# Gate/up stage of a two-layer encoder: left operands, right sides and products of its first units in another order

## The chip, the cores and the metric

The kernel runs on one core of a Trainium2 chip. Its time is the device time of one execution in microseconds. The engines are named as the profile names them: PE is TensorE (matmuls; PEld is its loading of weights), DVE is VectorE, ACT is ScalarE, POOL is GpSimd, and SP is SyncE, which here only issues DMAs.

## The reference

Two layers, each with an attention part and a SwiGLU part, on a sequence of 1024 tokens with 1024 features, all in float32. The change lies in the part below; the attention part only delivers `concat(y_tok, y_mem)`. D_FF is 2816.

```python
def rmsnorm(x, g):
    x32 = x.astype(jnp.float32)
    y = x32 * lax.rsqrt(jnp.mean(x32 * x32, axis=-1, keepdims=True) + EPS)
    return (y * g.astype(jnp.float32)).astype(x.dtype)
...
    for i in range(DEPTH):
        ...
        x = x + jnp.concatenate([y_tok, y_mem], axis=-1) @ w_out[i]
        h = rmsnorm(x, norm_ffn[i])
        gu = h @ w_gate_up[i]
        x = x + (jax.nn.silu(gu[..., :D_FF]) * gu[..., D_FF:]) @ w_down[i]
    return rmsnorm(x, norm_final)
```

## The kernel before

Activations lie transposed: a tile `x[m][f]` holds 128 features (m = 0..7) by 512 tokens (f = 0, 1). A float32 operand is split in two parts of a type that PE takes, `hi` (a cast on ACT, L106) and `lo` (the rest, a subtraction on DVE, L109), and a product is the sum of three matmuls, hi·hi, hi·lo and lo·hi.

Behind the attention each layer has three stages. The **output projection** makes `x[m][f]` for both halves of the tokens, eight products of 24 matmuls for each half. Its weights `wo` are loaded into raw buffers (tag `raw`, five of them, shared with the later stages) and split into left operands (tag `whl`, three buffers). In the second half each product is also followed by the normalizing of one tile of the first half and by its split into `hB`, the right sides B[0] and B[1].

The **gate/up stage** has 22 units (class `Pair`). A unit makes 128 rows of gate and 128 of up, as a product of a 2 by 2 block matrix (g1, g2, u1, u2) with a 2 by 2 block matrix (b11, b12, b21, b22), in seven products instead of eight (Strassen in Winograd's form). Product n takes a left operand and a right side B[n]:

- n = 0, 1: g1 and g2, with b11 and b21
- n = 2, 3: S2 = u1 + u2 - g1 and S1 = u1 + u2, with T2 = b22 - T1 and T1 = b12 - b11
- n = 4, 5: S3 = g1 - u1 and S4 = g2 - S2, with T3 = b22 - b12 and b22
- n = 6: u2, with T4 = T2 - b21

A product is 12 matmuls into a PSUM bank: 0, 2, 4 and 6 into the unit's `X`, 1, 3 and 5 into a `Y`, of which there are three. `read(n)` takes the result out: ACT copies `X` or a `Y`, or DVE adds it to an earlier copy. `prepare(n)` makes the left operands of n and n + 1 in one tile `wgu` of tag `whl`: for n = 0 from the raw gate weights, for n = 2 and 4 from a tile `wS` (tag `S`, two buffers) that POOL fills in two operations of 128 x 512, for n = 6 from u2. Each of the two raw tiles of a unit is 512 KB; after n = 4 and n = 6 a call of `load_gu` issues a next one on SP.

`right_sides()` normalizes the second half of the tokens: the sums of squares are finished (on PE, `st`), a power is taken on POOL (`nr`, L217), PE spreads it to all partitions (`bc`), and DVE scales the tiles x[k][1] by it. It then makes T2, T1, T3, b22 and T4 in this order, each for four blocks k, as `hT` or `hB`; a call of `run_some(rest, 3)` does three of its 20 steps.

The order of the products is a list: products 0 and 1 of units 0 to 3 (which need B[0] and B[1] alone), then products 2 to 6 of unit 0, of unit 1, of unit 2, of unit 3, then units 4 to 21, seven products each. `gate_up()` goes through the list; `prepare` runs four entries ahead. The order of instructions on an engine is set by a scheduler that goes by the order of the program and by what is ready, and is fixed when the kernel is built. All of the first left operands, five loads and four calls of `prepare`, stand in the program behind the output projection.

The **down stage** follows; its right sides come from DRAM tiles that `hand_over` writes after every second unit.

Of the kernel before, what the change touches and what calls it, by code (L numbers as in the profile page):

```python
# [17 lines left out]
P = 128  # L18
# [23 lines left out]
def trunk_kernel(ctx: ExitStack, tc: tile.TileContext, a: dict, out: bass.AP):  # L42
# [62 lines left out]
    def hi(dst, src):  # L105
        nc.scalar.copy(dst, src)  # L106
# [224 lines left out]
    for layer in range(2):  # L331
# [427 lines left out]
        with tc.tile_pool(name=f"fp{layer}", bufs=1, reuse_waits="tile") as fp:  # L759
# [27 lines left out]

            for m in range(3):
                load_x(m, 0)
            for f in range(2):  # L790
                for m in range(NK):
# [17 lines left out]
                    if f == 1:  # L809
                        k = next(parts)  # L810
                        B[k // 4][k % 4] = pair(x[k][0], h_op(k))

            def right_sides():

                bc = norms[1].scale()
                sub = lambda o, p_, q_: nc.vector.tensor_tensor(o, p_, q_, op=ALU.subtract)
                for k in range(4):
                    b11, b12, b21, b22 = x[k][0], x[k][1], x[k + 4][0], x[k + 4][1]
                    for i, t in ((k, b12), (k + 4, b22)):
                        nc.vector.scalar_tensor_tensor(  # L820
                            t, t, gains[:, 2 + layer, i : i + 1], bc, op0=ALU.mult, op1=ALU.mult
                        )
                    sub(b11, b12, b11)
                    t2 = temp("t2")
                    sub(t2, b22, b11)
                    B[2][k] = pair(t2, t_op(k))
                    sub(b21, t2, b21)
                    yield
                for k in range(4):
                    B[3][k] = pair(x[k][0], t_op(k))  # L830
                    yield
# [4 lines left out]
                for k in range(4):  # L836
                    B[5][k] = pair(x[k + 4][1], h_op(k))
                    yield
                for k in range(4):
                    B[6][k] = pair(x[k + 4][0], h_op(k))  # L840
                    yield

            class Pair:


                def __init__(self, j):
                    self.j = j
                    self.left, self.raw = {}, {}

                def prepare(self, n):  # L850

                    if n % 2 == 1:
                        return
                    g1, g2 = self.raw[0][:, :HS], self.raw[0][:, HS:]
                    if n > 0:
                        u1, u2 = self.raw[1][:, :HS], self.raw[1][:, HS:]
                    sub = lambda o, p_, q_: nc.gpsimd.tensor_tensor(o, p_, q_, op=ALU.subtract)
                    s = self.raw[0]
# [10 lines left out]
                    if n == 6:  # L869
                        hi(w[:, 0, :HS], u2)  # L870
                        lo(w[:, 1, :HS], u2, w[:, 0, :HS])
                    else:
                        hi(w[:, 0], s)
                        lo(w[:, 1], s, w[:, 0])
                    self.left[n], self.left[n + 1] = w[:, :, :HS], w[:, :, HS:]
                    if n > 3:
                        load_gu()

                def product(self, n):
                    if n == 0:  # L880
                        self.X = (
                            ps_s.tile([P, HS], F32, tag="S", name="X")
                            if self.j % 2
                            else ps_mm.tile([P, HS], F32, tag="mm", name="X")
                        )
                    if n in (1, 3):
                        self.Y = ps_t.tile([P, HS], F32, tag="T", name="Y")
                    ps, w = (self.Y if n in (1, 3, 5) else self.X), self.left[n]
                    for k in range(4):
                        kw = (w[:, 0, k * P : (k + 1) * P], w[:, 1, k * P : (k + 1) * P])  # L890
                        for i, (l, r) in enumerate(three(kw, (B[n][k][:, 0], B[n][k][:, 1]))):
                            nc.tensor.matmul(  # L892
                                ps, l, r, start=n in (0, 1, 3, 6) and k == 0 and i == 0,
                                stop=k == 3 and i == 2, skip_group_check=True,
                            )

                def read(self, n):
                    X, Y = self.X, getattr(self, "Y", None)
                    add = lambda o, p_, q_, op=ALU.add: nc.vector.tensor_tensor(o, p_, q_, op=op)  # L899
# [64 lines left out]
            for _ in range(5):  # L964
                load_gu()
# [301 lines left out]
```

## Time and profile before

| | |
|---|---|
| time, median of 3 runs (lowest to highest) | 2222.61 us (2220.63 to 2223.34) |
| time of the profiled execution | 2225.55 us |
| its span (first to last instruction) | 2223.8 us |
| mean granted clock of PE | 0.983 of full speed |
| PE busy | 2134.8 us, 96% |
| PEld busy | 1751.2 us, 79% |
| DVE busy | 1515.4 us, 68% |
| ACT busy | 1058.1 us, 48% |
| POOL busy | 692.1 us, 31% |

Busy time is the union of an engine's instructions; weight loads run beside matmuls and have their own line. A share is a mean over all stages of both layers. A wait is idle time of an engine directly ahead of an instruction, put down to the instruction that released it. The times in the rows further on count from the start of the span. In the timelines a row gathers neighbouring instructions of one kind, with the start of the first and the time that they took together.

### The profile page before, as it was taken

To read this page: it belongs to the slowest core of one execution; us is meant where nothing else is said; L and a number is where in the kernel's file an instruction comes from. 1 tells how busy PE (TensorE), PEld (TensorE's weight loads), DVE (VectorE), ACT (ScalarE), POOL (GpSimd) and SP (SyncE) were. 2 spreads that over 40 slices of the span, in tenths; PEclk is the share of its full clock that TensorE was granted. 3 is DMA by queue.
4 is the path that set the end of the run, shared out by engine and by line. 5 is a ranking of instruction groups with operands and counts; after the bars stand their busy time and mean duration, and the time that the engine had idled before them with its cause. 6 is when DMAs were issued, how large, how long until landed. Compare 5 with 4: busy or idle time off the path is not lost.

```text
span 2223.8 us, 28171 instructions
## 1 busy us (share of the span) xinstructions
PE 2134.8 (96%) x9930; PEld 1751.2 (79%) x9930; DVE 1515.4 (68%) x2241; ACT 1058.1 (48%) x2016; POOL 692.1 (31%) x647
## 2 busy tenths in 40 slices
PE   6899999899999999999999999999999999999996
PEld 6788888778888887787778888887788888877775
DVE  5677786776656665767866666667866566657575
ACT  5477784443333333445466566644433333334442
POOL 5334330143323330363233223201433333303540
PEclk9999999989999999999999999999999999999998
DMA  6312118223323236756332222282233332366562
GB/s 232 105 53 73 43 58 284 85 90 109 108 97 113 87 114 227 246 200 216 112 101 69 76 68 74 62 277 91 90 106 108 100 107 92 110 231 227 174 225 89
DMA packets 116444, 285.11 MB, mean 128 GB/s; under 512 B 12240, under 2 KB 18640, under 8 KB 116304
## 3 DMA queue, kind: packets, MB, share of 16 engines
q1 hardware_dynamic: 109968, 271.79, 36.5%
q10 hardware_dynamic: 6336, 11.54, 1.4%
q8 instruction: 78, 1.28, 0.2%
q14 instruction: 62, 0.51, 0.1%
HBM read 208.30 MB, written 68.94 MB: 125 GB/s over the span
## 4 chain that ended last, share of the span: by engine, by line
PE 39%; DVE 4%; issue 3%; ACT 2%; DMA 2%; POOL 1%; SPq 0%; POOLq 0%; DVEq 0%; ACTq 0%
PE X L892 10%; PE mm L139 8%; PE Y L892 8%; PE po L139 4%; PE X L1116 2%; PE Y L1116 2%; PE S L524 2%; PE O L587 2%; DMA b_raw<-b_d 1%; PE pT L567 1%; DVE hB L109 1%; DVE wd L109 1%; ACT wd L106 0%; ACT p L539 0%; DVE sq L202 0%
## 5 line engine op out<-in xcount | busy, mean ns | idle before, releaser
L892 PE MATMUL X<-hT,wgu 128*128 128x512 f32 x1056 | 265.5, 399 | 5.6 <-ACT wgu L106 4.0
L892 PE MATMUL Y<-hB,wgu 128*128 128x512 f32 x1056 | 257.8, 392 | 10.7 <-DVE g L899 10.7
L1116 PE MATMUL X<-hB,wd 128*128 128x512 f32 x1056 | 249.2, 396 | 8.2 <-ACT hB L106 3.6
L892 PE MATMUL X<-hB,wgu 128*128 128x512 f32 x1056 | 251.6, 393 | 0.0
L892 PEld LDWEIGHTS X<-hT,wgu 128*128 128x128 f32 x1056 | 200.3, 190 | 55.2 <-ACT wgu L106 4.8
L1116 PEld LDWEIGHTS X<-hB,wd 128*128 128x128 f32 x1056 | 200.8, 191 | 54.3 <-ACT hB L106 4.4
L892 PEld LDWEIGHTS Y<-hB,wgu 128*128 128x128 f32 x1056 | 199.1, 189 | 55.0 <-DVE g L899 11.6
L862 POOL TENSOR_TENSOR wS<-wgu_raw 128x512 f32<-128x512 f32 x44 | 73.0, 1659 | 536.0 <-issue 416.9
L552 POOL TENSOR_SCALAR p<-p,stat 128x384 f32<-128x384 f32 (+1 forms) x256 | 140.9, 570 | 309.8 <-DVE stat L549 206.7
L892 PEld LDWEIGHTS X<-hB,wgu 128*128 128x128 f32 x1056 | 200.3, 190 | 43.0 <-DVE wgu L109 1.3
L139 PE MATMUL mm<-hT,wqk 128*128 128x512 f32 x672 | 200.0, 405 | 0.1
L1116 PE MATMUL Y<-hB,wd 128*128 128x512 f32 x792 | 183.6, 392 | 9.3 <-DVE hB L109 4.5
L109 DVE TENSOR_TENSOR wgu<-wgu_raw,wgu 128x1024 fp32r<-128x1024 f32 (+1 forms) x88 | 98.6, 1121 | 135.1 <-ACT wgu L106 135.1
L139 PE MATMUL po<-yT,wo 128*128 128x512 f32 x768 | 184.7, 394 | 0.0
L1116 PEld LDWEIGHTS Y<-hB,wd 128*128 128x128 f32 x792 | 149.4, 189 | 42.5 <-DVE hB L109 5.3
L109 DVE TENSOR_TENSOR hB<-b_raw,hB 128x512 fp32r<-128x512 f32 x154 | 130.5, 884 | 63.0 <-ACT hB L106 62.8
L106 ACT CAST wgu<-wS 128x1024 fp32r<-128x1024 f32 x88 | 92.5, 1051 | 156.9 <-PE Y L892 104.8
L139 PEld LDWEIGHTS po<-yT,wo 128*128 128x128 f32 x768 | 142.4, 188 | 29.6 <-issue 1.0
L109 DVE TENSOR_TENSOR wgu<-wS,wgu 128x1024 fp32r<-128x1024 f32 x88 | 146.9, 1670 | 25.2 <-ACT wgu L106 25.2
L106 ACT CAST wgu<-wgu_raw 128x1024 fp32r<-128x1024 f32 (+1 forms) x88 | 73.4, 834 | 181.6 <-PE Y L892 131.7
L106 ACT CAST hB<-b_raw 128x512 fp32r<-128x512 f32 x154 | 88.9, 619 | 104.3 <-DMA b_raw<-b_d 104.1
L539 ACT ACTIVATE p<-p,stat 128x256 f32<-128x256 f32 (+1 forms) x192 | 112.3, 586 | 51.3 <-DVE stat L535 48.8
(162 smaller groups left out, 4053.6 us busy)
## 6 DMA issues: line engine op xcount, KB each, us to landing
wgu_raw<-in_w_gu SPq DMA_DIRECT2D x88, 512.0 KB
b_raw<-b_d SPq DMA_DIRECT2D x70, 512.0 KB
wd_raw<-in_w_dn SPq DMA_DIRECT2D x50, 512.0 KB
b_d<-c SPq DMA_DIRECT2D x88, 256.0 KB
b_d<-t SPq DMA_DIRECT2D x66, 256.0 KB
wo_raw<-in_w_out SPq DMA_DIRECT2D x32, 512.0 KB
wd_kept<-in_w_dn SPq DMA_DIRECT2D x10, 1024.0 KB
x<-in_x SPq DMA_DIRECT2D x32, 256.0 KB
```

What stands on the lines that cost most here:

```text
L106: nc.scalar.copy(dst, src)
L109: (eng or nc.vector).tensor_tensor(dst, src, h.bitcast(F32), op=ALU.subtract)
L139: nc.tensor.matmul(ps[:, :n], l, r, start=start and i == 0 and j == 0, stop=stop and i == len(order) - 1 and j == 2,)
L524: nc.tensor.matmul(s_[:, :n], Q[self.h][:, qb * P : (qb + 1) * P], k, start=j == 0, stop=j == 1)
L539: nc.scalar.activation(p[:, :n], p[:, :n], AF.Exp, bias=m1, scale=-1.0, accum_out=s1)
L552: nc.gpsimd.tensor_scalar(p[:, :n], p[:, :n], ri[:, i : i + 1], 1.0, op0=ALU.mult, op1=ALU.mult)
L567: nc.tensor.transpose(tr[:, j * P : (j + 1) * P], p[:, j * P : (j + 1) * P], ident)
L587: nc.tensor.matmul(o[:, c0 : c0 + w * P], self.value(j), t[:, s0 : s0 + w].rearrange("p j q -> p (j q)"), start=j == js[0] and t is self.p ...
L862: nc.gpsimd.tensor_tensor(s[:, HS:], u1, u2, op=ALU.add)
L892: nc.tensor.matmul(ps, l, r, start=n in (0, 1, 3, 6) and k == 0 and i == 0, stop=k == 3 and i == 2, skip_group_check=True,)
L1116: nc.tensor.matmul(bank, l, r, start=i in (0, 1, 3, 6) and p == 0 and n == 0, stop=p == HF - 1 and n == 2, skip_group_check=True,)
```

## The change

The class `Pair`, the list of units and the list of loads move ahead of the output projection. In the second half of the projection (f = 1) the loop also loads gate and up weights and, at m = 2 to 5, calls `prepare(0)` of units 0 to 3; these four operands lie in tiles `wgu8` of tag `t8` instead of `whl`. The up weights of units 0 and 1 are loaded there too; units 2 and 3 load their gate weights a second time later.

`prepare` rounds n down to an even number and returns where that operand has been made. For n = 4 it doesn't take a new `wS` tile: S3 and S4 overwrite S1 and S2 in the tile of n = 2, S4 in place, in halves that are swapped.

`right_sides` goes in the order T1, T2, b22, T3, T4. A tile of the second half is scaled where it is first needed (x[k][1] for T1, x[k+4][1] for T2); T2 takes the place of T1 in x[k][0] instead of a temporary tile. One of its steps runs ahead of the first product, then one after each of the first eight products and two after each later one.

The order of products 2 to 6 of the early units goes by pairs, units 0 and 1 and then units 2 and 3: product 3 of both, then 2, 5, 4, 6 of both. In `read` the multiplication of c2 by g2 stands with whichever of products 4 and 5 comes last. The number of matmuls, casts, subtractions and right sides is what it was.

```diff
+                def prepare(self, n):
+
+                    n -= n % 2
+                    if n in self.left:
+                        return
 ...
-                    if n in (2, 4):
-                        s = fp.tile([P, D], F32, tag="S", name="wS", bufs=2)
-                    if n == 2:
-                        nc.gpsimd.tensor_tensor(s[:, HS:], u1, u2, op=ALU.add)
-                        sub(s[:, :HS], s[:, HS:], g1)
-                        self.s2 = s[:, :HS]
-                    if n == 4:
-                        sub(s[:, :HS], g1, u1)
-                        sub(s[:, HS:], g2, self.s2)
-                    w = wp.tile([P, 2, D], F32R, tag="whl", name="wgu", bufs=3)
+                    if n == 2:
+                        self.s = fp.tile([P, D], F32, tag="S", name="wS", bufs=2)
+                    if n in (2, 4):
+                        s = self.s
+                    if n == 2:
+                        nc.gpsimd.tensor_tensor(s[:, HS:], u1, u2, op=ALU.add)
+                        sub(s[:, :HS], s[:, HS:], g1)
+                    if n == 4:
+                        sub(s[:, HS:], g1, u1)
+                        sub(s[:, :HS], g2, s[:, :HS])
+                    if n == 0 and self.j < first:
+                        w = fp.tile([P, 2, D], F32R, tag="t8", name="wgu8", bufs=6)
+                    else:
+                        w = wp.tile([P, 2, D], F32R, tag="whl", name="wgu", bufs=3)
 ...
+                    if n == 4:
+                        self.left[4], self.left[5] = self.left[5], self.left[4]
-                    if n > 3:
+                    if n > 3 or (n == 0 and 2 <= self.j < first):
                         load_gu()
 ...
                         add(self.c2, self.c2, self.c1)
+                        if 5 in self.seen:
+                            add(self.c2, self.c2, self.g2, ALU.mult)
 ...
-            order += [(u, n) for u in us[:first] for n in range(2, 7)]
+            for j in range(0, first, 2):
+                order += [(u, n) for n in (3, 2, 5, 4, 6) for u in us[j : j + 2]]
-            loads = [(u, 0) for u in us[:first]] + [(u, 1) for u in us[:first]]
-            loads += [(u, i) for u in us[first:] for i in range(2)]
+            loads = [(us[j], 0) for j in range(first)] + [(us[0], 1), (us[1], 1)]
+            loads += [(u, i) for u in us[2:] for i in range(2)]
 ...
                         B[k // 4][k % 4] = pair(x[k][0], h_op(k))
+                        if 1 <= m <= 2:
+                            load_gu()
+                        if 2 <= m < 2 + first:
+                            if m == 4:
+                                load_gu()
+                            if m == 3:
+                                load_gu()
+                            us[m - 2].prepare(0)
 ...
+                for k in range(4):
+                    t = x[k][0]
+                    sub(t, normalized(k), t)
+                    B[3][k] = pair(t, t_op(k))
+                    yield
+                for k in range(4):
+                    t, b21 = x[k][0], x[k + 4][0]
+                    sub(t, normalized(k + 4), t)
+                    B[2][k] = pair(t, t_op(k))
+                    sub(b21, t, b21)
+                    yield
+                for k in range(4):
+                    B[5][k] = pair(x[k + 4][1], h_op(k))
+                    yield
 ...
-            for _ in range(5):
-                load_gu()
-            lead = 4
-            for u, n in order[:lead]:
-                u.prepare(n)
+            lead = 4
+            rest = right_sides()
 ...
             def gate_up():
+                run_some(rest, 1)
+                load_gu()
 ...
-                    if i < 2 * first:
-                        run_some(rest, 3)
                     u.product(n)
                     u.read(n)
+                    run_some(rest, 1 if i < 2 * first else 2)
```

What this does to the engines' fixed orders, at three places of layer 0. In the rows a name left of the arrow is written, names right of it are read, and a number behind a name tells tiles of one name apart.

PE before, from the sixth product of the stage on (products 0 and 1 of the early units, then the first that take T2, `hT_4551` and `hT_4568`, and T1, `hT_4595` and `hT_4618`):

```order
L892 MATMUL Y<-hB,wgu 128x512 x12
L892 MATMUL X<-hB,wgu 128x512 x2
L892 MATMUL X<-hT_4551,wgu 128x512 x2
L892 MATMUL Y<-hB,wgu 128x512 x2
L892 MATMUL X<-hB,wgu 128x512 x10
L892 MATMUL Y<-hB,wgu 128x512 x10
L892 MATMUL Y<-hT_4595,wgu 128x512 x2
L892 MATMUL X<-hT_4551,wgu 128x512 x4
L892 MATMUL X<-hT_4568,wgu 128x512 x6
L892 MATMUL Y<-hT_4595,wgu 128x512 x4
L892 MATMUL Y<-hT_4618,wgu 128x512 x6
L892 MATMUL X<-hT_4624,wgu 128x512 x2
```

PE now, from the fifth product on (`wgu_4410` and `wgu_4454` are the first operands of units 2 and 3; `hT_4553` and `hT_4594` are T1, `hT_4633` and `hT_4686` T2):

```order
L844 MATMUL X<-hB,wgu_4410 128x512 x12
L844 MATMUL Y<-hB,wgu_4410 128x512 x12
L844 MATMUL X<-hB,wgu_4454 128x512 x12
L844 MATMUL Y<-hB,wgu_4454 128x512 x12
L844 MATMUL Y<-hT_4553,wgu 128x512 x6
L844 MATMUL Y<-hT_4594,wgu 128x512 x6
L844 MATMUL Y<-hT_4553,wgu 128x512 x6
L844 MATMUL Y<-hT_4594,wgu 128x512 x6
L844 MATMUL X<-hT_4633,wgu 128x512 x6
L844 MATMUL X<-hT_4686,wgu 128x512 x6
L844 MATMUL X<-hT_4633,wgu 128x512 x6
L844 MATMUL X<-hT_4686,wgu 128x512 x6
```

Products 0 and 1 of all four units now stand whole ahead of any product with a T, and product 3 of two units comes ahead of their product 2.

DVE before, where the T2 of layer 0 end and the T1 are split (`g1_4585` is the sum that reads unit 0's first `Y`, `wgu_4615` the first operand of unit 3, the `x` written by L816 first T2's and later T3's terms):

```order
L816 TENSOR_TENSOR x_3924<-x_4179,x_3924 128x512
L109 TENSOR_TENSOR hT8_4568<-t2_4566,hT8_4568 128x512
L816 TENSOR_TENSOR t2_4590<-x_4355,x_3924 128x512
L109 TENSOR_TENSOR hT8_4595<-x_3918,hT8_4595 128x512
L816 TENSOR_TENSOR x_4026<-t2_4590,x_4026 128x512
L109 TENSOR_TENSOR hT8_4568<-t2_4590,hT8_4568 128x512
L109 TENSOR_TENSOR hT8_4595<-x_3920,hT8_4595 128x512
L899 TENSOR_TENSOR g1_4585<-Y_4600,g1_4585 128x512
L109 TENSOR_TENSOR wgu_4615<-wgu_raw_4519,wgu_4615 128x1024
L109 TENSOR_TENSOR hT8_4618<-x_3922,hT8_4618 128x512
L109 TENSOR_TENSOR hT8_4618<-x_3924,hT8_4618 128x512
L816 TENSOR_TENSOR x_4063<-x_4233,x_4063 128x512
```

DVE now, from the first scaling of the right sides on (L936 scales, L933 subtracts, `hT8_4553` and `hT8_4594` are T1; `g1_4571` and `g1_4610` read the first `Y` of units 0 and 1):

```order
L936 SCALAR_TENSOR_TENSOR x_4063<-x_4063,gains_104,bc_4549 128x512
L936 SCALAR_TENSOR_TENSOR x_4100<-x_4100,gains_104,bc_4549 128x512
L933 TENSOR_TENSOR x_3918<-x_4063,x_3918 128x512
L933 TENSOR_TENSOR x_3920<-x_4100,x_3920 128x512
L852 TENSOR_TENSOR g1_4571<-Y_4577,g1_4571 128x512
L109 TENSOR_TENSOR hT8_4553<-x_3918,hT8_4553 128x512
L109 TENSOR_TENSOR hT8_4553<-x_3920,hT8_4553 128x512
L936 SCALAR_TENSOR_TENSOR x_4142<-x_4142,gains_104,bc_4549 128x512
L936 SCALAR_TENSOR_TENSOR x_4179<-x_4179,gains_104,bc_4549 128x512
L933 TENSOR_TENSOR x_3922<-x_4142,x_3922 128x512
L933 TENSOR_TENSOR x_3924<-x_4179,x_3924 128x512
L852 TENSOR_TENSOR g1_4610<-Y_4616,g1_4610 128x512
```

Before, the first of these sums stands behind 26 operations of the right sides; now behind four. No low part of a `wgu` stands between them.

POOL before, from the power of the first half's norm (`nr_4222`) past that of the second half (`nr_4539`); `wS_4667` and `wS_4721` belong to unit 0:

```order
L217 TENSOR_TENSOR nr_4222<-nv_4221,neg_half_109 128x4
L862 TENSOR_TENSOR wS_4667<-wgu_raw_4521 128x512
L857 TENSOR_TENSOR wS_4721<-wgu_raw_4513,wgu_raw_4521 128x512
L857 TENSOR_TENSOR wS_4667<-wS_4667,wgu_raw_4513 128x512
L857 TENSOR_TENSOR wS_4721<-wgu_raw_4513,wS_4667 128x512
L217 TENSOR_TENSOR nr_4539<-nv_4538,neg_half_109 128x4
L862 TENSOR_TENSOR wS_4784<-wgu_raw_4727 128x512
L857 TENSOR_TENSOR wS_4784<-wS_4784,wgu_raw_4515 128x512
```

POOL now, the same stretch; `wS_4637`, `wS_4663` and `wS_4873` belong to units 0, 1 and 2, and the second power is `nr_4544`:

```order
L803 TENSOR_TENSOR wS_4663<-wS_4663,wgu_raw_4316 128x512
L803 TENSOR_TENSOR wS_4637<-wgu_raw_4273,wgu_raw_4413 128x512
L803 TENSOR_TENSOR wS_4637<-wgu_raw_4273,wS_4637 128x512
L803 TENSOR_TENSOR wS_4663<-wgu_raw_4316,wgu_raw_4457 128x512
L803 TENSOR_TENSOR wS_4663<-wgu_raw_4316,wS_4663 128x512
L810 TENSOR_TENSOR wS_4873<-wgu_raw_4733 128x512
L803 TENSOR_TENSOR wS_4873<-wS_4873,wgu_raw_4556 128x512
L217 TENSOR_TENSOR nr_4544<-nv_4543,neg_half_109 128x4
L810 TENSOR_TENSOR wS_4895<-wgu_raw_4829 128x512
```

Ahead of the second power stood four operations on weights, of unit 0; now ten stand there, the last two of them for S1 and S2 of unit 2. S3 and S4 of a unit go into the tile of its S1 and S2.

## Rows read from the trace of the kernel before

**Rows 1.** Waits of PE: engine, tile, line, releaser: us in total, times, longest us

```profile
PE Y L892 <- DVE g L899: 10.7, 2, 5.3
...
PE X L892 <- ACT wgu L106: 4.0, 2, 3.3
...
PE X L892 <- DVE wgu L109: 1.6, 2, 1.3
```

**Rows 2.** Windows: window, us, busy us (count) of each engine, clock, DMA share, GB/s

```profile
418.62:437.83 19.21, 18.60 (x83) 14.64 (x82) 14.97 (x24) 7.28 (x10) 1.02 (x1) 1.00 0.04 14
437.83:469.50 31.67, 23.07 (x75) 17.21 (x74) 28.65 (x37) 17.40 (x29) 12.90 (x6) 0.78 0.10 34
513.29:532.58 19.29, 19.29 (x85) 15.77 (x84) 13.52 (x14) 7.07 (x10) 6.60 (x4) 1.00 0.35 124
1552.57:1582.21 29.64, 21.79 (x75) 15.67 (x74) 28.27 (x37) 17.39 (x29) 7.04 (x4) 0.83 0.06 17
```

**Rows 3.** Timeline of PE, layer 0: start, us, instruction, count, [wait, releaser]

```profile
418.62 4.01 PE L892 MATMUL X<-hB,wgu 128*128 128x512 f32 x17
...
437.83 0.61 PE L892 MATMUL X<-hB,wgu 128*128 128x512 f32 x2
...
444.26 1.22 PE L892 MATMUL Y<-hB,wgu 128*128 128x512 f32 x2 [5.35 <-DVE g L899]
...
461.24 5.49 PE L892 MATMUL X<-hT,wgu 128*128 128x512 f32 x12 [3.25 <-ACT wgu L106]
...
510.57 5.60 PE L892 MATMUL X<-hB,wgu 128*128 128x512 f32 x24
516.01 2.88 PE L892 MATMUL Y<-hB,wgu 128*128 128x512 f32 x12
```

**Rows 4.** Timeline of PE, layer 1, the same places

```profile
1533.36 4.01 PE L892 MATMUL X<-hB,wgu 128*128 128x512 f32 x17
...
1552.57 0.62 PE L892 MATMUL X<-hB,wgu 128*128 128x512 f32 x2
...
1628.73 2.88 PE L892 MATMUL Y<-hB,wgu 128*128 128x512 f32 x12
```

**Rows 5.** Timeline of DVE and POOL behind the stage's start, layer 0

```profile
419.96 1.23 DVE L109 TENSOR_TENSOR wgu<-wgu_raw,wgu 128x1024 fp32r<-128x1024 f32 x1 [0.44 <-ACT wgu L106]
...
423.96 1.02 POOL L217 TENSOR_TENSOR nr<-nv,neg_half 128x4 f32<-128x4 f32 x1 [8.92 <-DVE nv L216]
...
426.92 1.41 DVE L820 SCALAR_TENSOR_TENSOR x<-x,gains,bc 128x512 f32<-128x512 f32 x2 [1.22 <-PE bc L226]
...
444.12 1.22 DVE L109 TENSOR_TENSOR wgu<-wgu_raw,wgu 128x1024 fp32r<-128x1024 f32 x1
...
453.06 3.70 DVE L109 TENSOR_TENSOR hB<-x,hB 128x512 fp32r<-128x512 f32 x6
```

**Rows 6.** POOL's subtractions by line (ns: least/median/most), and timelines at units 0 and 5

```profile
L857 POOL TENSOR_TENSOR wS<-wgu_raw x44: 1282/1677/2282, 409.7 to 1939.1; 128x512 f32<-128x512 f32 x44
...
L857 POOL TENSOR_TENSOR wS<-wgu_raw,wS x44: 1290/1730/1748, 413.8 to 1940.7; 128x512 f32<-128x512 f32 x44
...
452.77 5.14 POOL L862 TENSOR_TENSOR wS<-wgu_raw 128x512 f32<-128x512 f32 x1 [27.79 <-DVE wgu L109]
...
551.86 1.63 POOL L862 TENSOR_TENSOR wS<-wgu_raw 128x512 f32<-128x512 f32 x1 [12.25 <-issue]
...
554.79 0.59 ACT L902 COPY g<-X 128x512 f32<-128x512 f32 x1 [1.59 <-PE X L892]
...
557.31 2.95 PE L892 MATMUL X<-hT,wgu 128*128 128x512 f32 x12
```

**Rows 7.** Timelines: cast of a `wo` operand on ACT, and a load and its first use

```profile
402.56 1.05 ACT L106 CAST wo<-wo_raw 128x1024 fp32r<-128x1024 f32 x1 [3.86 <-PE po L139]
...
463.52 0.88 SPq L962 DMA_DIRECT2D wgu_raw<-in_w_gu  x2
...
467.16 1.29 POOL L862 TENSOR_TENSOR wS<-wgu_raw 128x512 f32<-128x512 f32 x1 [3.67 <-DMA wgu_raw<-in_w_gu]
```

More of the change, by code (lines that the diff above doesn't have):

```diff
@@ new lines, in trunk_kernel @@
+            us = [Pair(j) for j in range(NF)]
+            first = 4
+            order = [(u, n) for u in us[:first] for n in (0, 1)]
+            for j in range(0, first, 2):
+                order += [(u, n) for n in (3, 2, 5, 4, 6) for u in us[j : j + 2]]
+            order += [(u, n) for u in us[first:] for n in range(7)]
+            loads = [(us[j], 0) for j in range(first)] + [(us[0], 1), (us[1], 1)]
+            loads += [(u, i) for u in us[2:] for i in range(2)]
+            loads = iter(loads)
@@ L788, in trunk_kernel, with load_gu @@
+            def load_gu():
+                u, i = next(loads, (None, 0))
+                if u is not None:
+                    u.raw[i] = raw_tile("wgu_raw")
+                    nc.sync.dma_start(u.raw[i], a["w_gu"][layer, 2 * u.j + i])
             for m in range(3):
@@ L816, in right_sides, with normalized @@
                 sub = lambda o, p_, q_: nc.vector.tensor_tensor(o, p_, q_, op=ALU.subtract)
-                for k in range(4):
[L818 to L827, printed above, removed]
+                def normalized(i):
+                    nc.vector.scalar_tensor_tensor(
+                        x[i][1], x[i][1], gains[:, 2 + layer, i : i + 1], bc, op0=ALU.mult, op1=ALU.mult
+                    )
+                    return x[i][1]
+                for k in range(4):
+                    t = x[k][0]
+                    sub(t, normalized(k), t)
+                    B[3][k] = pair(t, t_op(k))
                     yield
                 for k in range(4):
-                    B[3][k] = pair(x[k][0], t_op(k))
+                    t, b21 = x[k][0], x[k + 4][0]
[5 more added lines that the diff above has]
+                    B[5][k] = pair(x[k + 4][1], h_op(k))
                     yield
@@ L946, in hand_over @@
                 keep(6, p, o)
-            us = [Pair(j) for j in range(NF)]
-            first = 4
-            order = [(u, n) for u in us[:first] for n in (0, 1)]
-            order += [(u, n) for u in us[:first] for n in range(2, 7)]
-            order += [(u, n) for u in us[first:] for n in range(7)]
-            loads = [(u, 0) for u in us[:first]] + [(u, 1) for u in us[:first]]
-            loads += [(u, i) for u in us[first:] for i in range(2)]
-            loads = iter(loads)
-            def load_gu():
-                u, i = next(loads, (None, 0))
-                if u is not None:
-                    u.raw[i] = raw_tile("wgu_raw")
-                    nc.sync.dma_start(u.raw[i], a["w_gu"][layer, 2 * u.j + i])
-            for _ in range(5):
-                load_gu()
             lead = 4
-            for u, n in order[:lead]:
-                u.prepare(n)
             rest = right_sides()
             def gate_up():
+                run_some(rest, 1)
+                load_gu()
                 for i, (u, n) in enumerate(order):
```

125 lines of the change are left out of this document (60 added, 65 removed).

## The prediction

> **What bounds the kernel now.** I read the waits of PE first: in the gate/up stage it stood 10.7 us, in two waits, for an addition of VectorE (DVE) into `g`, and 5.6 us for left operands `wgu` [rows 1]. Two waits means one for each layer, so the loss sits at one place of a layer. The windows show where. The first 19.2 us of the stage run at full clock with PE at 18.60 of 19.21; the next 31.7 us have PE at 23.07, a mean granted clock of 0.78, which is a mix of the levels 1.2 and 2.4 GHz, and DVE busy 28.65 us; a later unit of 19.29 us has PE busy throughout [rows 2]. Layer 1 has the same hole (21.79 of 29.64, clock 0.83). So PE bounds the stage except in one stretch behind its start, which DVE sets.
>
> PE's own timeline says what it costs. Two products (24 matmuls) start at 510.57 and the next at 516.01, so a product takes 2.72 us; the first of these two ends the four early units, and unit 4 starts at 513.29 [rows 3]. The stage starts at 418.62: the four early units took 94.67 us. Four units at the later pace are 4 x 19.29 = 77.16 [rows 2]. Layer 1: start 1533.36, unit 4 at 1628.73 - 2.72 = 1626.01, so 92.65 us [rows 4]. The losses are 17.5 and 15.5 us. Of each, the first six products hold 2.9 (19.21 instead of 6 x 2.72 = 16.32, in both layers [rows 3, 4]): the sums of squares and the broadcast of the norm, which stay. What is left for the change is 94.67 - 19.21 - (77.16 - 16.32) = **14.6 us in layer 0 and 12.6 in layer 1**.
>
> Where these went: PE waits 5.35 us at 444.26 because the addition that frees a Y bank stands on DVE behind the right sides, and the left operand of unit 3 gets its low part only at 444.12 [rows 3, 5]. At 461.24 it waits again, 3.25 us, for a cast of S2, and the twelve matmuls behind take 5.49, twice their later 2.72, at the lower clock [rows 3].
>
> **The change part by part.**
>
> *Left operands of units 0 to 3 during the projection.* Four casts and four subtractions move ahead of the stage; in their old places stand the casts of S2 of units 0 and 1 and S3 of unit 0, which have no wait left. Low parts also leave the stretch in which DVE is the bound, such as that of unit 3 at 444.12 [rows 5]. Cost ahead: four times 1.05 on ScalarE (ACT) and 1.23 on DVE [rows 5, 7], beside a projection in which PE was never idle. The cover there is the lead of `wo`: the cast at 402.56 waited 3.86 us for PE to free its buffer [rows 7]; with 1.05 and 1.23 behind it, its operand is ready near 404.9 and used at 418.62 - 5.44 = 413.2, so 8.3 us ahead. The new loads take four of five raw buffers, so the last three `wo` loads go through one buffer in turn. A turn is the load (two were issued from 463.52 to 464.40, the data of the later was used at 467.16 [rows 7]; about 3 us), 1.05, 1.23 and about 0.7 of handing over: 6 us against PE's 5.44. Counting back three products from 404.9, the first of these turns begins near 388.6; the third ends near 406.6, still 6.6 us ahead. I price this at nothing. Two repeated loads for units 2 and 3 (512 KB each) fall into a stretch with a DMA share of 0.04 to 0.10 [rows 2]: nothing.
>
> *Right sides begun with T1.* The count is the same (44 operations of DVE, 0.62 us each by six in 3.70 us [rows 5], 27 us in all); only the order changes. They start 8.30 us after the stage's start [rows 3, 5]. The four T1 with two additions are 14 operations: done 17.0 after the start. PE needs them after eight products, 19.21 + 5.44 = 24.65. T2 with two additions is 18 more: 28.2, needed from 24.65 + 5.6 = 30.2. The four b22: 30.7, needed at 35.8. T3 and one subtraction for a left operand: 36.9, needed at 41.3. T4: about 40, needed at 46.8. The thinnest margin is 2.0 us, at T2, and its last quarter is needed 2 us later still. So DVE, today the bound, drops behind PE. Next late would be T2.
>
> *Pairs.* Two units take product 3, then 2, 5, 4, 6 in turn. A Y bank is freed by an addition that now stands between right sides: that of unit 0 comes fifth, after two scalings and two T1 differences, 2.5 us into them, and PE needs the bank 13 us later. Each left operand gets its buffer two products or more before its use, 5.4 us against 1.05 + 1.23. ACT copies c1 of the second unit about 1 us before PE overwrites X: no stall, but little room.
>
> *The norm behind two operations of GpSimd (POOL).* The power for the norm started at 423.96, when its input came [rows 5]. In the new order unit 2's sum and difference for S2 stand ahead of it, and they wait for the low part that ends at 419.96 + 1.23 = 421.2 [rows 5]. Two operations at 1.28 to 1.68 end at 423.8 to 424.6: the power comes 0 to 0.7 us later, and with it everything behind. I take **0.4 us in each layer**, the middle. Their data are in place: PE frees the buffer for S2 of unit 0 at 418.62 - 2 x 5.44 = 407.7; cast, subtraction and two POOL operations end near 413.4 and release the raw buffer, and a load of 3 us lands near 416.4.
>
> *S3 and S4 overwrite S2.* In the 18 later units of each layer the two subtractions for S3 and S4 can start only when DVE has read S2, at 551.86, where today an operation starts on the same release. They last 1.677 and 1.730 at the median [rows 6], so 555.27; the cast takes it to 556.32, the copy of X behind it on ACT (0.59) to 556.91. PE overwrites X at 557.31 [rows 6]. Today that copy starts at 554.79. So 0.40 us of room are left of 1.9, in every later unit: nothing, but the closest cover in the change. With the longest of the 44, 2.282 and 1.748, it is 0.22 late [rows 6].
>
> The Trainium skill (SBUF — State Buffer, "Who interferes with whom") says that a DVE instruction with two SBUF inputs and a GpSimd instruction that reads SBUF exclude each other, the later one blocking until the first is through. By that each subtraction waits for at most one DVE operation; those that stand there take 0.62, so 1.28 + 0.62 = 1.90 each and the copy ends at 557.30: the room is gone and nothing lost, 2196. Behind one of 1.23 it would be 0.60 late in 36 units, 2218. The medians of this trace lie below the first of these; one row of 5.14 beside six DVE operations [rows 5, 6] lies above both.
>
> **The sum.** 14.6 + 12.6 - 2 x 0.4 = 26.4 us. The profiled execution took 2225.55 (span 2223.8): 2199.1. It lies 0.13% above the median of 2222.61; scaled, **2196.2 us**.
>
> **The rivals.**
> (a) *POOL becomes the bound of the later units.* If the two subtractions take 3.41 + 0.40 = 3.81 together PE starts to wait, in 36 units. At 4.55 (0.73 late, 26.4/36) the gain is gone; above it the kernel is slower: with 5.0 for both, 1.19 late, 43 us, 2239. For it: the 0.40 us, the 5.14 row. Against: that row is one of 44, and medians and maxima of the two operations that count stay below 4.03 [rows 6].
> (b) *DVE keeps the early units.* Beside POOL six subtractions would take longer; at 0.8 instead of 0.62, the 32 operations up to T2 are 5.8 later, 2 to 4 of which the margins take: about 3 us in each layer, 2202; at 1.0, 12 later, about 8 us: 2212. Against: between the power and the end of T3 no POOL operation can run in the new order, since unit 3's S2 waits for a buffer that DVE frees among the last T3 operations.
> (c) *The projection starves.* With 6 us for each of the three loads in turn the last operand comes at 415.9, 2.7 late: 2202. Against: my count leaves 6.6 us of room, and a wait of PE for `wo` is not in this trace.
> (d) *The change does less than it says:* the first left operands are late again, because a cast waits for its load. Half the gain: 2209. Against: the loads precede the casts by 10 us.
>
> **How the numbers follow.** Forecast, 2193 to 2199: 0.70. Rivals (b) and (c): 0.12, 2200 to 2212. (a) with small lateness, up to the 2218 above: 0.08; (a) at or beyond break-even: 0.06, two thirds of it slower. (d): 0.04. Leaving out 0.2 gives 2192 to 2207: the lower end is the forecast with no delay of the norm and a little of the 2.9 us returned, the upper takes in most of (b) and (c). About 0.2% is what a measurement here can tell from no change, 4.4 us. Faster: 0.91, same 0.05, slower 0.04.
>
> **What would show it.** PE without a wait of over 1 us between the stage's start and unit 4, clock 1.00 there, unit 4 about 80.5 us after the start in both layers; `g` and `wgu` gone from PE's waits in this stage. The power 0 to 0.7 us later relative to the start. The copy of g1 starting near 556.3 on the old time axis, some 0.4 us or more before PE's third product; a wait of PE for that copy, at one place in every unit, would be (a). A wait of PE for `wo` would be (c), one for `hT8` (b). The prediction is wrong if the four early units take over 85 us or if a later unit takes over 19.4.

## The result and the profile after

The changed kernel takes **2203.52 us** (median of 6 runs, 2201.36 to 2206.16) against 2221.62 for the kernel before, measured beside it: a ratio of 0.9919, 95% interval 0.9908 to 0.993, or 18 us less (15.6 to 20.4). The sign and the range were right; the forecast of 2196.2 was 7 us too low. The profiled execution took 2205.49, its span is 2202.5.

The waits of PE (columns as in [rows 1]) no longer hold `g` or `wgu` in the gate/up stage. The line of the waits for sums of squares, in which this stage has a share, has grown; the trace of before had 10.7 us in 5 waits.

```profile
PE st L211 <- DVE sq L202: 12.2, 6, 4.6
```

The windows (columns as in [rows 2]) answer to the hole of [rows 2]. The first two are the first six products of layers 0 and 1, the third the stretch from there to unit 4 in layer 0, the last a later unit:

```profile
421.80:442.28 20.48, 18.98 (x84) 14.68 (x83) 16.23 (x25) 9.94 (x15) 4.41 (x4) 1.00 0.12 38
1524.43:1546.07 21.64, 20.40 (x84) 15.24 (x82) 16.43 (x25) 10.25 (x16) 4.42 (x4) 0.92 0.13 37
...
442.28:503.18 60.90, 60.90 (x265) 49.61 (x264) 47.77 (x64) 27.20 (x44) 15.26 (x10) 1.00 0.28 88
...
580.33:599.62 19.29, 19.29 (x86) 15.77 (x84) 11.31 (x14) 7.08 (x10) 5.95 (x5) 1.00 0.35 123
```

The hole is closed: from the sixth product to unit 4 PE is busy throughout, at full clock, and takes 60.90 us in each layer, where it took 75.46 and 73.44 (from the starts in [rows 3, 4]: 513.29 - 437.83, 1626.01 - 1552.57). That gives 14.6 and 12.5 us. But the first six products, 19.21 before in both layers, now take 20.48 and 21.64. Together unit 4 starts 81.4 and 82.5 us behind the stage's start, where the forecast had 80.5.

PE's timeline at the start of both stages shows where: a wait of 0.90 for `sq` that was not there, and in layer 1, behind it, a stretch at half the clock (six matmuls in 1.88 us instead of 1.62, the broadcast in 2.08 instead of 1.12). The first row is that of the kernel before in layer 0, without a wait; the others are the changed kernel's.

```profile
422.66 1.02 PE L211 MATMUL st<-inv_d,sq 128*128 128x1 f32 x8
...
421.80 4.12 PE L844 MATMUL X<-hB,wgu 128*128 128x512 f32 x17
426.82 1.02 PE L211 MATMUL st<-inv_d,sq 128*128 128x1 f32 x8 [0.90 <-DVE sq L202]
427.71 1.62 PE L844 MATMUL Y<-hB,wgu 128*128 128x512 f32 x6
429.93 1.12 PE L226 MATMUL bc<-diag,ones 128*128 128x512 f32 x2 [0.60 <-DVE diag L219]
...
1529.45 1.02 PE L211 MATMUL st<-inv_d,sq 128*128 128x1 f32 x8 [0.90 <-DVE sq L202]
1530.34 1.88 PE L844 MATMUL Y<-hB,wgu 128*128 128x512 f32 x6
1532.56 2.08 PE L226 MATMUL bc<-diag,ones 128*128 128x512 f32 x2 [0.34 <-DVE diag L219]
```

DVE and POOL at the same place point to the cause. Two additions of squares took 1.41 us before (first row); now they take 2.38 (the second alone 1.66 instead of 0.69), and beside them runs POOL's sum for S2 of unit 2. The power (`nr`) starts 0.25 behind the start of its input `nv`; POOL's queue is clear by then.

```profile
421.10 1.41 DVE L202 TENSOR_TENSOR sq<-sq 128x512 f32<-128x512 f32 x2
...
424.30 2.38 DVE L202 TENSOR_TENSOR sq<-sq 128x512 f32<-128x512 f32 x2
...
425.02 1.66 DVE L202 TENSOR_TENSOR sq<-sq 128x512 f32<-128x512 f32 x1
...
427.88 0.17 DVE L216 TENSOR_SCALAR nv<-st 128x4 f32<-128x4 f32 x1 [1.21 <-PE st L211]
...
424.46 1.67 POOL L810 TENSOR_TENSOR wS<-wgu_raw 128x512 f32<-128x512 f32 x1 [2.53 <-DVE wgu L109]
426.20 1.60 POOL L803 TENSOR_TENSOR wS<-wS,wgu_raw 128x512 f32<-128x512 f32 x1
428.13 1.02 POOL L217 TENSOR_TENSOR nr<-nv,neg_half 128x4 f32<-128x4 f32 x1 [0.33 <-DVE nv L216]
```

### The profile page after: what moved, and what is told of

Same layout as the page of the kernel before. It is cut to its first block, busy times and chain, and to the rows that moved or that the text cites. A ratio compares the mean times of both kernels' runs of the same rounds, so it can differ in the third digit from the quotient of the medians.

```text
span 2202.5 us, 28160 instructions
## 1 busy us (share of the span) xinstructions
PE 2129.8 (97%) x9930; PEld 1749.9 (79%) x9930; DVE 1440.2 (65%) x2241; ACT 1056.5 (48%) x2016; POOL 673.9 (31%) x647
## 3 DMA queue, kind: packets, MB, share of 16 engines
q8 instruction: 78, 1.28, 0.2%
## 4 chain that ended last, share of the span: by engine, by line
PE 73%; issue 10%; DVE 6%; ACT 4%; DMA 4%; POOL 3%; SPq 0%; POOLq 0%; DVEq 0%; ACTq 0%
PE X L844 21%; PE Y L844 16%; PE mm L139 13%; PE X L1136 6%; PE po L139 4%; PE S L524 3%; PE Y L1136 3%; PE O L587 3%; PE pT L567 2%; DMA b_raw<-b_d 1%; DVE hB L109 1%; ACT p L539 1%; POOL x L1096 1%; DVE wd L109 1%; DMA wd_kept<-in_w_dn 1%
## 5 line engine op out<-in xcount | busy, mean ns | idle before, releaser
L844 PE MATMUL X<-hT,wgu 128*128 128x512 f32 x1056 | 259.0, 395 | 0.0
L109 DVE TENSOR_TENSOR wgu<-wgu_raw,wgu 128x1024 fp32r<-128x1024 f32 (+1 forms) x88 | 85.7, 974 | 190.3 <-ACT wgu L106 190.3
L803 POOL TENSOR_TENSOR wS<-wgu_raw 128x512 f32<-128x512 f32 x44 | 73.6, 1672 | 379.0 <-DVE wgu L109 379.0
L109 DVE TENSOR_TENSOR wgu<-wS,wgu 128x1024 fp32r<-128x1024 f32 x88 | 109.7, 1247 | 62.6 <-ACT wgu L106 62.6
L810 POOL TENSOR_TENSOR wS<-wgu_raw 128x512 f32<-128x512 f32 x44 | 58.3, 1326 | 251.2 <-DMA wgu_raw<-in_w_gu 197.5
```

What stands on the lines that cost most here:

```text
L109: (eng or nc.vector).tensor_tensor(dst, src, h.bitcast(F32), op=ALU.subtract)
L844: nc.tensor.matmul(ps, l, r, start=n in (0, 1, 3, 6) and k == 0 and i == 0, stop=k == 3 and i == 2, skip_group_check=True,)
```

## The experiments

All are edits of the changed kernel unless said otherwise. The gain in the table is against the median of before that ran beside each (2221.5 to 2224.9). "Six" is the time of the first six products, "rest" from there to unit 4, both from PE's starts, for layers 0 / 1. The intervals of the gains reach 2.4 to 5.5 us either way, so a gap between two gains of less than some 3 us is not told from none. Rows with one run are single profiled executions: they are read by their traces, not by their times.

| kernel | median us (runs) | gain us | six us | rest us |
|---|---|---|---|---|
| before, second trace | 2226.13 (1) | | 19.26 / 19.24 | 75.42 / 73.45 |
| changed | 2203.52 (6) | 18.1 | 20.48 / 21.64 | 60.91 / 60.91 |
| changed, again | 2203.65 (4) | 19.0 | 20.53 / 21.61 | 60.92 / 60.96 |
| power first | 2204.31 (6) | 20.6 | 19.51 / 19.51 | 60.96 / 60.96 |
| t8 tiles lower | 2208.18 (6) | 16.7 | 21.64 / 21.52 | 60.99 / 60.92 |
| no early operands | 2212.64 (6) | 12.2 | 20.28 / 20.29 | 64.04 / 64.05 |
| no pairs | 2213.82 (6) | 11.1 | 20.44 / 21.95 | 63.66 / 63.66 |
| T2 first | 2206.48 (6) | 15.1 | 21.28 / 21.42 | 60.96 / 60.99 |
| T1 first alone | 2224.56 (12) | -3.0 | 20.30 / 20.28 | 72.62 / 72.59 |
| pools on 512 bytes | 2194.75 (4) | 26.8 | 20.21 / 20.98 | 59.84 / 59.84 |
| both edits | 2191.60 (4) | 29.9 | 19.27 / 19.28 | 59.84 / 59.84 |
| t8 at 256 past 512 | 2199.90 (1) | | 20.23 / 21.33 | 59.84 / 59.84 |
| longer subtractions | 2241.86 (1) | | 20.48 / 21.50 | 60.91 / 60.95 |

**The power first** (e_power)

```diff
+            self.power = r
 ...
                         self.s = fp.tile([P, D], F32, tag="S", name="wS", bufs=2)
+                        if self.j == 2:
+                            sub(self.s[:, HS : HS + 4], norms[1].power, norms[1].power)
```

> Edit: the tile for S1 and S2 of unit 2 is first written by a small POOL operation that reads the power of the norm, so that POOL's sum and difference for it stand behind the power and not ahead of it; all other engines keep their order. Theory A (DVE's second addition of the squares took 1.66 us instead of 0.69 because POOL's sum for unit 2 ran beside it, and that made the norm 0.97 us late in each layer): the addition is back at 0.69, PE has no wait for st of 0.9, and the first six products take 19.21 + 0.4 = 19.6 us in both layers instead of 20.48 and 21.64; in layer 1 the fall of the granted clock behind the wait goes too. Time 2203.5 - 2 to 3 = 2201. Theory B (the order on POOL's queue alone delays the power, by the 0.33 us that the row of the power shows): the gain is 0.3 us in each layer, the additions stay at 1.66, time 2203.

DVE, PE and POOL at the stage's start of layer 0 in this kernel:

```profile
424.25 1.41 DVE L202 TENSOR_TENSOR sq<-sq 128x512 f32<-128x512 f32 x2
...
425.81 1.02 PE L211 MATMUL st<-inv_d,sq 128*128 128x1 f32 x8
...
427.11 1.02 POOL L217 TENSOR_TENSOR nr<-nv,neg_half 128x4 f32<-128x4 f32 x1 [5.22 <-DVE nv L216]
...
428.99 1.27 POOL L813 TENSOR_TENSOR wS<-wgu_raw 128x512 f32<-128x512 f32 x1
```

Theory A holds in the trace: the additions are back at 1.41, the first six products take 19.51 in both layers, and no wait for `st` stands in the stage. The edit also takes POOL's work out of the queue ahead of the power; but the additions stand ahead of the power, so that queue can't have slowed them. 0.97 us of each layer was DVE's addition beside POOL, and 1.16 more in layer 1 the clock. POOL paid too: its sum takes 1.27 here, with DVE idle, where it took 1.67. In the timed runs these 3.1 us don't show by themselves: the gain is 20.6 against 18.1 and 19.0, and the time, 2204.31, is not the expected 2201. The pair of runs with aligned pools, below, shows 3.15 (2194.75 and 2191.60), at the edge of what is told.

**Early operands undone** (e_late): the four operands go back to tag `whl` and behind the projection.

```diff
-                    if n == 0 and self.j < first:
-                        w = fp.tile([P, 2, D], F32R, tag="t8", name="wgu8", bufs=6)
 ...
-                            us[m - 2].prepare(0)
 ...
+            for _ in range(5):
+                load_gu()
             lead = 4
+            for u, n in order[:lead]:
+                u.prepare(n)
```

> Undoes the first part alone: the first left operands go back into the three whl buffers and stand behind the projection; T1 first and pairs stay. Theory A (the pairs and the new order of the right sides carry the gain, since by count DVE has no margin left but loses little: three low parts of 1.23 us between the right sides, T2 complete near 30.6 us behind the stage's start and needed from 29.8): waits of PE of 1 to 3 us in each layer, no delay of the norm, the first six products 19.21: 2202 to 2207. Theory B (the left operands carry the gain): unit 4 starts 5 us or more later in each layer than in the changed kernel (81.4 and 82.6 us behind the stage's start there), 2214 or more.

The rest takes 3.1 us more in each layer: theory A by the trace, while the time of 2212.64 lies between the ranges of both. Six products at 20.28 were not expected by either. Here POOL's sum starts beside DVE's `diag`, which takes 1.75 instead of 0.69, and PE waits 1.64 for it (0.59 before). It is the effect that e_power removed, at another instruction. Against e_power the two stages take 7.7 us more in the traces, and the gain is 8.3 less. The last row is one of the waits in the rest.

```profile
427.60 1.26 POOL L810 TENSOR_TENSOR wS<-wgu_raw 128x512 f32<-128x512 f32 x1
...
427.66 1.75 DVE L219 TENSOR_TENSOR diag<-ident,nr 128x512 f32<-128x512 f32 x1 [1.13 <-POOL nr L217]
...
429.47 1.12 PE L226 MATMUL bc<-diag,ones 128*128 128x512 f32 x2 [1.64 <-DVE diag L219]
...
451.10 3.02 PE L841 MATMUL Y<-hT,wgu 128*128 128x512 f32 x12 [1.14 <-DVE g L849]
```

**Pairs undone** (e_nopairs)

```diff
-            for j in range(0, first, 2):
-                order += [(u, n) for n in (3, 2, 5, 4, 6) for u in us[j : j + 2]]
+            order += [(u, n) for u in us[:first] for n in (3, 2, 5, 4, 6)]
 ...
-                    run_some(rest, 1 if i < 2 * first else 2)
+                    run_some(rest, 1 if i < 2 * first else 3)
```

> Undoes the pairs alone: units 0 to 3 take products 3, 2, 5, 4, 6 one unit after the other (with three steps of the right sides behind each product from the ninth on, else product 4 would stand ahead of its right side). By the count of DVE, T3 of all blocks is ready 36.9 us behind the stage's start plus the 0.97 us of the norm, and unit 0 would take it at 33.7; T4 at 41, wanted from 36.5. Theory A (the pairs give DVE the time that it lacks): PE waits 3 to 5 us in each layer, the clock falls for a window: 2211 to 2215. Theory B (the T1-first order and the early operands suffice): no wait over 1 us, 2203.5.

PE's timeline: product 4 of unit 0 waits for both halves of T3, 0.72 and 0.91 us. The rest takes 2.75 more in each layer, a little less than theory A said, and the clock does not fall there.

```profile
456.03 0.73 PE L844 MATMUL X<-hT,wgu 128*128 128x512 f32 x2 [0.72 <-DVE hT L109]
...
458.37 0.51 PE L844 MATMUL X<-hT,wgu 128*128 128x512 f32 x1 [0.91 <-ACT hT L106]
```

**The order of the right sides undone** (e_t2): the body of `right_sides` of the kernel before, in the steps of the changed one.

```diff
-                order += [(u, n) for n in (3, 2, 5, 4, 6) for u in us[j : j + 2]]
+                order += [(u, n) for n in (2, 3, 5, 4, 6) for u in us[j : j + 2]]
```

> Undoes the order of the right sides alone: T2 of all blocks with its normalizing first, then T1, T3, b22, T4 as in the kernel before, and the early pairs take product 2 ahead of 3; early left operands and pairs stay. Theory A (by count T2 is complete after 28 operations of DVE of 0.62 us each behind 8.3 + 1.0 us, so at 26.7 us, and its first half some 5 us sooner; PE wants it from 26.1): the order itself carries little, waits of 0 to 2 us in each layer, 2203 to 2208. Theory B (T1 first is what frees PE): 5 us or more lost in each layer, 2214 or more.

Theory A: the rest is the same to 0.1 us, and PE has no wait in it. T1 first carries nothing where the other two parts stand.

**The order of the right sides alone** (e_right): the edits of e_late and e_nopairs together.

> Does the order of the right sides alone: first left operands in whl behind the projection and no pairs, so two parts undone together. Undone singly these cost 3.1 and 2.75 us a layer in the early units. Theory A (each part gives the same few microseconds, the rest of the 13.5 us a layer comes from T1 first and from products 0 and 1 of all units standing whole ahead of any T): the two losses add to about 6 us a layer, unit 4 some 88 us behind the stage's start, 2217 to 2221. Theory B (early operands and pairs stand in for each other): the loss is nearly that of the kernel before, unit 4 at 93 us or later, 2222.

Theory B. PE's timeline of layer 0 shows the hole of before again, at T2: waits of 1.90 and 1.99, and three matmuls in 2.05.

```profile
452.37 0.50 PE L841 MATMUL X<-hT,wgu 128*128 128x512 f32 x1 [1.90 <-ACT hT L106]
452.70 0.40 PE L841 MATMUL Y<-hB,wgu 128*128 128x512 f32 x1
455.09 2.05 PE L841 MATMUL X<-hT,wgu 128*128 128x512 f32 x3 [1.99 <-DVE hT L109]
```

Undone singly, the two parts cost 3.1 and 2.75 us a layer; undone together 11.7 (72.6 - 60.9). They stand in for each other: either closes most of the hole, and only the last 3 us need both.

**The cover of S3 and S4** (e_longer)

```diff
                         sub(s[:, HS:], g1, u1)
+                        if self.j >= first:
+                            sub(s[:, HS:], g1, u1)
```

> Edit of the changed kernel: in the 18 later units of each layer the first subtraction for S3 is done twice, one POOL operation of 1.67 us more; the result is the same. In the trace of the changed kernel the copy of g1 ends 0.57 us before PE overwrites X in each of these units. Theory A (this room is all the cover there is): PE waits 1.67 - 0.57 = 1.1 us in each of 36 units for that copy, a unit takes 20.4 us, about 2243. Theory B (the chain has more slack elsewhere and starts sooner): the unit stays at 19.29, 2203.

First the changed kernel in a later unit, then this one. In the first the copy of g1 ends at 584.61 + 0.58 = 585.19 and PE overwrites X at 585.77: 0.58 us of room.

```profile
580.25 1.67 POOL L803 TENSOR_TENSOR wS<-wgu_raw 128x512 f32<-128x512 f32 x1 [9.38 <-DVE wgu L109]
...
581.41 1.07 DVE L852 TENSOR_TENSOR c<-c,g 128x512 f32<-128x512 f32 x1
581.89 1.73 POOL L803 TENSOR_TENSOR wS<-wgu_raw,wS 128x512 f32<-128x512 f32 x1
582.51 1.66 DVE L970 TENSOR_TENSOR t<-c,t 128x512 f32<-128x512 f32 x1
...
584.61 0.58 ACT L855 COPY g<-X 128x512 f32<-128x512 f32 x1
...
585.77 2.95 PE L844 MATMUL X<-hT,wgu 128*128 128x512 f32 x12
```

```profile
PE X L846 <- ACT g L857: 28.6, 36, 1.2
```

PE now waits in each of the 36 units, and four of them take 81.30 instead of 77.15, 1.04 more each: 38 us in all, of which 28.6 are the waits and the rest slower matmuls directly behind them. Theory A: 0.6 us is the whole cover.

The waits alternate, and show what POOL pays beside DVE. In one unit the added subtraction runs beside operations of DVE and takes 1.74 us, in the next DVE is idle and it takes 1.28:

```profile
626.99 1.74 POOL L803 TENSOR_TENSOR wS<-wgu_raw 128x512 f32<-128x512 f32 x1
627.50 1.78 DVE L972 TENSOR_TENSOR c<-c,c 128x512 f32<-128x512 f32 x1
...
630.34 3.06 PE L846 MATMUL X<-hT,wgu 128*128 128x512 f32 x12 [1.01 <-ACT g L857]
...
647.56 1.28 POOL L803 TENSOR_TENSOR wS<-wgu_raw 128x512 f32<-128x512 f32 x1
...
650.46 3.05 PE L846 MATMUL X<-hT,wgu 128*128 128x512 f32 x12 [0.56 <-ACT g L857]
```

**Where the 2.79 us come from** (e_low, e_align, e_256). Every product with an operand in tag `t8`, T1 to T3 or an early `wgu8`, takes 2.79 to 2.80 us from start to start, every other 2.72. First the place was tried:

```diff
-        raw = raw_tile(f"{name}_raw")
-        nc.sync.dma_start(raw, src)
         w = pool.tile([P, 2, D], F32R, tag=tag, name=name, bufs=bufs)
+        raw = raw_tile(f"{name}_raw")
+        nc.sync.dma_start(raw, src)
```

> Edit: the tiles of tag t8 are laid ahead of the raw tiles in the pool, 20,480 bytes lower in each partition; the order of all instructions is the same. In the changed kernel every product with an operand in tag t8 takes 2.79 to 2.80 us and every other 2.72. Theory A (the place in SBUF sets it, by a border between 108,032, the end of the tiles read at 2.72, and 128,896, the first t8 tile, or a bit above): T1 at 141,184 and 149,376 stays slow, T2 lies half at 132,992 and half at 116,608, T3 at 124,800 and 108,416, so of a later unit product 3 stays at 2.80, product 2 comes to about 2.76 and product 4 to 2.72 to 2.76; the first operands of units 1 and 3 (116,608 and 108,416) go to 2.72, that of unit 0 (132,992) stays at 2.79. A unit goes from 19.29 to about 19.18; with 44 units 4 to 5 us: 2199. Theory B (traffic of the other engines in that pool, or the form of the tile): all stay at 2.79 to 2.80, time 2203.5.

Theory A fell: products 2, 3 and 4 of a later unit stay at 2.79, 2.80 and 2.80, a unit at 19.29. From start to start e_low takes 2.72 for product 1 and 2.79 for product 2:

```profile
582.25 2.88 PE L844 MATMUL Y<-hB,wgu 128*128 128x512 f32 x12
584.97 2.95 PE L844 MATMUL X<-hT,wgu 128*128 128x512 f32 x12
587.76 2.96 PE L844 MATMUL Y<-hT,wgu 128*128 128x512 f32 x12
```

Next the remainder of the address:

```diff
+    sp = pool("sp", bufs=1)
     hp = pool("hp", bufs=16)
     wp = pool("wp", bufs=1)
-    sp = pool("sp", bufs=1)
 ...
-                    stat = sp.tile([P, 4, 4], F32, tag="stat", name="stat", bufs=4)
+                    stat = ap.tile([P, 8, 4], F32, tag="stat", name="stat", bufs=4)
```

(and `sink` with `nsink`, `inv_d` with `neg_half`, `nv` with `nr` share a tile each)

> Edit of the changed kernel: the small tiles move so that every pool begins at a multiple of 512 bytes of a partition (the pool of the stages stood 384 bytes past one; the tiles of hB, wgu and yT, read at 2.72 us a product, stood on one); the order of every engine stays the same. Moving the t8 tiles 20,480 bytes down, a multiple of 512, had changed nothing. Theory A (an operand that doesn't begin on such a multiple costs PE some 0.006 us a matmul): products with T1, T2, T3 or the early operands go from 2.79 or 2.80 to 2.72, a later unit from 19.29 to 19.04; 36 units x 0.25 + 8 early units x 0.4 is 12 us: 2192 or, with a gain in the attention stage, whose tiles stood at the same remainder, less. Theory B (form of the tile or traffic): 2.80 stays, 2203.5.

> Edit of the kernel with all pools on multiples of 512 bytes: 256 bytes are left free ahead of the pool of the stages, so that T1 to T3 and the early operands begin 256 bytes past such a multiple, hB and wgu stay on one; the order of every engine stays the same. Theory A (512 bytes count): products with T or an early operand are back at 2.79 to 2.80, about 2203. Theory B (256 bytes suffice): all products 2.72, a later unit 19.04, about 2194.

A later unit's first products, then its window, in e_align; and the window in e_256:

```profile
580.34 2.88 PE L844 MATMUL Y<-hB,wgu 128*128 128x512 f32 x12
583.05 2.88 PE L844 MATMUL X<-hT,wgu 128*128 128x512 f32 x12
585.77 2.88 PE L844 MATMUL Y<-hT,wgu 128*128 128x512 f32 x12
...
577.62:596.66 19.04, 19.04 (x86) 15.77 (x85) 11.30 (x14) 7.08 (x10) 5.95 (x5) 1.00 0.38 125
```

```profile
576.90:595.94 19.04, 19.04 (x85) 15.77 (x84) 11.30 (x14) 7.08 (x10) 5.95 (x5) 1.00 0.34 125
```

All products take 2.72, a unit 19.04 instead of 19.29, and so also with 256 bytes left over (theory B of e_256). The changed kernel's t8 tiles begin 128 bytes past a multiple of 256; a multiple of 256 is enough. The single time of e_256, 2199.90, is not the 2194 that theory B gave; its two gate/up stages are as short as those of e_align to 1.1 us in all, and the rest of the 5 us lies outside them.

**Both edits** (e_best)

> The two edits together: pools on multiples of 512 bytes, and the power of the norm ahead of unit 2's sum on POOL. By theory A of both: 2192 - 2.5 = 2189 or less. If the first edit does nothing: 2201 to 2204, as the second alone.

2191.60 us, 0.9866 of before (0.9853 to 0.9878): faster than both kernels, by 30 and some 12 us.

**Second traces** (r_after, r_before)

> The changed kernel once more, for a second trace. Gate/up by now expected as in the first: unit 4 at 20.48 or, with a fall of the granted clock behind the norm's wait, about 21.5 us plus 60.91 behind the stage's start in each layer; the parts before the first stage and the down stages differ by some 2 us either way, by where the clock falls. 2201 to 2206.

> The kernel before once more, for a second trace. If the first trace is typical, unit 4 starts 92 to 95 us behind the stage's start in both layers, and the first six products take 19.21; the part up to the output projection, 297.1 us in the first trace and 297.8 to 299.4 in those of the other kernels, comes out near 298.5. If the shortfall of the gain lies in the first trace, the early units lose less here.

The stage repeats to 0.1 us in both. So the losses read from the first trace of before were typical, and the shortfall is not there.

## Why the prediction was right, and where it fell short

- **What bounds the stage:** right. The 14.6 and 12.6 us that the hole was to give came as 14.6 and 12.5 from the sixth product to unit 4.
- **Which part carries it:** the text priced the parts together. The runs split them: early operands and pairs each do most of it alone, T1 first does nothing beside them (e_t2) and next to nothing alone (e_right).
- **The norm behind POOL: the step that failed.** The sum had 0.4 us a layer for the power waiting in POOL's queue. It does not wait there: it starts 0.25 us behind the start of its input, as before (0.24). It comes 0.99 us later behind the stage's start, not 0 to 0.7, because its input does. POOL's sum of unit 2 ran beside DVE's addition of the squares, and the two additions took 2.38 instead of 1.41 (e_power). The first six products grew by 1.27 us in layer 0 and 2.43 in layer 1, 2.9 more than the sum had; e_power gives back 0.97 and 2.13 of it. In the text's terms, the early start of POOL's work was priced as a place in a queue, not as work beside DVE, and the clock that falls behind a wait in the chain of the norm was not priced at all. 26.4 - 2.9 = 23.5 us is what the traces show in the stage (187.3 - 163.9 = 23.4).
- **The skill's rule, weighed at the wrong place.** The Trainium skill (SBUF — State Buffer, "Who interferes with whom") has a DVE instruction with two SBUF inputs and a GpSimd instruction that reads SBUF exclude each other, the later blocking. The text put the wait on POOL's subtractions alone. The trace agrees with the rule at the additions of the squares: POOL's sum ends at 424.46 + 1.67 = 426.13, and DVE's two additions end at 424.30 + 2.38 = 426.68, 0.55 behind it, 0.97 later than the 1.41 us that they take alone. In the later units both paid: DVE took 1.07 and 1.66 for operations of 0.68, and POOL 1.67 and 1.73 for subtractions, of which the first kind takes 1.28 with DVE idle (e_longer). The medians of before, on which the text put its 0.40 us of room, held that price already.
- **The early operands in `t8`, priced at nothing:** their products take up to 0.08 us more than 2.72. Most of the 0.30 us by which the first six products of e_power still exceed 19.21 is theirs: with aligned pools they take 19.27 against 19.51. The two behind add 0.07 each. [rows 2] held the hint: 19.29 for a unit is 0.25 more than seven times 2.72.
- **S3 and S4 in place:** right. The room was 0.58 instead of 0.40, no PE wait in 36 units, and the price of rival (a) had the right size (e_longer).
- **Rivals (b), (c), (d):** none came as described. PE has no wait for `hT8`, `wo` or `wgu`. But what (b) rested on, DVE slower beside POOL, did come, at the squares, ahead of the stretch where (b) looked for it. (By its own terms the last operand in (c) comes at 415.6, not 415.9.)
- **What stays open:** the traces of the stage show 23.4 us, the timed runs 18.1 and 19.0. In the layer-0 projection, ten traces with early operands have 113.8 to 117.8 us, 114.7 in the mean, against 113.9 in the four without: 0.8 that the sum had at nothing. Both profiled executions of before (2225.55 and 2226.13) lie 3.9 and 3.4 above its timed medians. Those of the changed kernel (2205.49 and 2199.49) lie 20.1 and 26.6 below them, 23.4 in the mean as in the stage, though the two differ too much to rest on that. The stretches outside the stage differ by 3 to 7 us between the fourteen traces. No run settles the rest.

## What to carry to other kernels

Work that moves to an idle engine is not free because that engine is idle: look for what runs beside it on DVE at its new place, above all in a short chain like a norm, where every step is on the path. Parts of a change that each fill the same hole don't add; undo them singly and together before saying which one is worth its code. Where two products of one form differ by a few per cent in the trace, ask where their operands lie.

## What the runs showed of the hardware

- PE took 2.79 to 2.80 us for a product with an operand that begins 128 bytes past a multiple of 256 in its partition, and 2.72 with all operands on such multiples; moving the pools alone gave some 9 us of 2203.
- A DVE addition of 128x512 with both inputs in SBUF took 1.66 us instead of 0.69 beside a POOL operation that read SBUF, and a POOL subtraction of that size took 1.74 instead of 1.28 beside DVE operations of that kind (e_longer).
- A wait of 0.9 us for `st` can cost twice itself. In the eight traces in which POOL ran beside the sum of squares, the granted clock fell to half within the first six products in 10 of 16 cases (in layer 1 always), at a price of some 0.8 to 1.5 us each. In the six traces without that wait it fell in none of 12, though in four of these (e_late and e_right) PE waited 1.63 to 1.66 us for `diag` a little later. So the length of a single wait does not decide it; what does was not tried.
